# The inner norms of a macaron layer: mean squares by two wide products and an inverse root by exponential and logarithm, in place of narrow sums, a diagonal and a square root

## The chip, the cores and the metric

The kernel runs on one core of one Trainium2 chip. The metric is the device time of one execution in microseconds (us). Engines are named TensorE (PE; its weight loads are PEld), VectorE (DVE), ScalarE (ACT), GpSimd (POOL) and SyncE (SP, which only issues transfers).

## What is computed

One layer over 512 tokens of width 1024, all in float32:

```python
def rmsnorm(x, g):
    y = x * lax.rsqrt(jnp.mean(x * x, axis=-1, keepdims=True) + 1e-6)
    return y * g

x = x + 0.5 * swiglu_ffn(rmsnorm(x, ffn1_norm), ...)      # norm 1, feed-forward width 2816
x = x + hybrid_mixer(rmsnorm(x, mix_norm), ...)           # norm 2, attention and pooling
x = x + 0.5 * swiglu_ffn(rmsnorm(x, ffn2_norm), ...)      # norm 3
x = rmsnorm(x, final_norm)                                # final norm
```

The first three are the inner norms. The final norm is not touched.

## The kernel before

The residual stream is held transposed: eight tiles x[k] of 128 channels by 512 tokens. Products of float32 precision are made of three products in the faster format float32r: each operand is split into a high part (a cast on ScalarE, line 132) and a low part (a subtraction on VectorE, line 133), and mm3 (line 193) adds high x high, high x low and low x high in PSUM. Its lines 198, 199 and 200 are most of TensorE's work.

The work has three stages in a row: the first feed-forward block (about 0 to 325 us), the mix stage (325 to 490) and the second feed-forward block (490 to the end). The feed-forward blocks use a block scheme with seven products instead of eight for most of their work; its sums of weights and of activations run on VectorE, ScalarE and through transfers.

An inner norm never scales x ahead of a product. The products take x times the norm's gain, and what comes out is multiplied per token by the inverse root of the token's mean square. For that the class Norm keeps acc, the sum over k of x[k] squared (128 partitions by 512 tokens: squares on ScalarE, additions on VectorE, lines 308 to 315, for norm 3 the jobs of lines 1695 to 1704). When it is complete:

- per_token (line 317, for norm 2 line 1149): four products of acc with a vector of ones give each token's sum as one column per 128 tokens, tokens on partitions; in float32 each is two instructions, so eight. ScalarE takes the square root (line 326 or 1161), a dummy activation (tables, line 226) loads the table set of the function that comes next, VectorE makes the inverse root r with one Newton step (rsqrt_of, line 285), four columns in all.
- The diagonal (line 332 or 1174): identity times r, 128 by 512.
- spread (line 339 or 1181): ones times the diagonal, two instructions of 512 columns, gives every partition the inverse root of all 512 tokens; ScalarE copies it to rb (line 342 or 1186).

rb is used where channels lie on partitions (gate and up values of the feed-forward blocks, lines 424 and 428; the block scheme's scaled x, line 365; the pooling input, line 1422); r where tokens do (q, k and v, lines 1312 and 1401).

In the feed-forward blocks, ffn_up (line 412) calls norm.finish() with high priority ahead of the last quarter of the products of its first four banks; the compiler's own scheduler orders the engines there. SyncE's transfers, and from line 579 on TensorE, VectorE and ScalarE, follow the written order. The first four banks are evacuated by lines 424 to 428 once rb is there; the blocks of line 397 follow on VectorE.

In the mix stage everything is a job with an engine, a cost, a rank, what it waits for and the banks and buffers that it gets and gives back. plan() (line 1002) replays these costs and writes down the order of every engine. The jobs of norm 2 (lines 1188 to 1193) have rank -1, ahead of nearly all others; line 1491 lets the first of them wait for sixteen products. The Sqrt table for norm 3 is loaded by a job behind the softmax (line 1706).

The dummy activation is what loads a table: an activation whose function isn't in the loaded set gets a load (ACT_TABLE_LOAD) in front.

Of the kernel before, what the change touches and what calls it, by code (L numbers as in the profile page):

```python
# [16 lines left out]
P = 128  # L17
# [14 lines left out]
MAGIC = 1597463007.0  # L32
REL = 257
# [23 lines left out]
def layer(  # L57
# [162 lines left out]
    ones = const.tile([P, P], F32, name="ones")  # L220
    table = const.tile([P, 1], F32, name="table")
    nc.vector.memset(ones, 1.0)
    eps = const.tile([P, 1], F32, name="eps")
    nc.vector.memset(eps, EPS)

    def tables(func, after):

        nc.scalar.activation(table, after, func, scale=0.0)


    tables(AF.Sqrt, ones[:, 0:1])
    idle = abank()
    for _ in range(8):
        nc.tensor.matmul(idle[:, :P], ones, ones, start=True, stop=True)
# [59 lines left out]
    class Norm:  # L294


        def __init__(self, which):
            self.which, self.h, self.acc = which, {}, None
# [9 lines left out]
        def square(self, k):  # L308
            if self.acc is None:
                self.acc = tpool.tile([P, S], F32, tag="acc", name=name("acc"), bufs=1)  # L310
                nc.scalar.activation(self.acc, x[k], AF.Square)
            else:
                sq = temp()
                nc.scalar.activation(sq, x[k], AF.Square)
                nc.vector.tensor_tensor(self.acc, self.acc, sq, op=ALU.add)

        def per_token(self, total, after=None):
            for t in range(NT):
                nc.tensor.matmul(
                    total[:, t : t + 1], self.acc[:, t * P : (t + 1) * P], ones[:, 0:1],  # L320
                    start=True, stop=True,
                )
            v, root, self.r = (
                small.tile([P, NT], F32, tag=what, name=name(what)) for what in ("v", "root", "r")
            )
            nc.scalar.activation(root, total[:, :NT], AF.Sqrt, scale=1.0 / D, bias=eps)
            if after:
                tables(after, root[:, 0:1])
            nc.vector.tensor_scalar(v, total[:, :NT], 1.0 / D, EPS, op0=ALU.mult, op1=ALU.add)
            rsqrt_of(v, root, self.r)  # L330
            self.diag = temp()
            nc.vector.tensor_tensor(
                self.diag.rearrange("p (t c) -> p t c", t=NT),
                ident.unsqueeze(1).to_broadcast([P, NT, P]),
                self.r.unsqueeze(2).to_broadcast([P, NT, P]),
                op=ALU.mult,
            )

        def spread(self, wide):
            nc.tensor.matmul(wide, ones, self.diag, start=True, stop=True)  # L340
            self.rb = small.tile([P, S], F32, tag="rb", name=name("rb"), bufs=1)
            nc.scalar.copy(self.rb, wide)

        def finish(self):
            self.per_token(abank(), AF.Silu)
            self.spread(abank())
# [309 lines left out]
    class Down:  # L656
# [154 lines left out]
        def product(self, acc, g, a, i, further=False, scale=None):  # L811
# [7 lines left out]
            if self.n_products == 12:  # L819
                tables(AF.Sqrt, a[0][:, 0, 0:1].bitcast(F32))  # L820
# [19 lines left out]
    n1, n2, n3 = Norm(0), Norm(1), Norm(2)  # L840
# [100 lines left out]
    with tc.tile_pool(name="mix", bufs=1, reuse_waits="tile") as mpool:  # L941
# [207 lines left out]
        def per_token():  # L1149
            for t in range(NT):  # L1150
                nc.tensor.matmul(
                    buf["total"][:, t : t + 1], n2.acc[:, t * P : (t + 1) * P], ones[:, 0:1],
                    start=True, stop=True,
                )

        n2_small = {}

        def root_of():
            for what in ("v", "root", "r"):
                n2_small[what] = small.tile([P, NT], F32, tag=what, name=name(what))  # L1160
            nc.scalar.activation(
                n2_small["root"], buf["total"][:, :NT], AF.Sqrt, scale=1.0 / D, bias=eps
            )
            tables(AF.Exp, n2_small["root"][:, 0:1])

        def reciprocal_root():
            v, n2.r = n2_small["v"], n2_small["r"]
            nc.vector.tensor_scalar(
                v, buf["total"][:, :NT], 1.0 / D, EPS, op0=ALU.mult, op1=ALU.add
            )  # L1170
            rsqrt_of(v, n2_small["root"], n2.r)

        def diagonal():
            nc.vector.tensor_tensor(
                buf["diag"].rearrange("p (t c) -> p t c", t=NT),
                ident.unsqueeze(1).to_broadcast([P, NT, P]),
                n2.r.unsqueeze(2).to_broadcast([P, NT, P]),
# [3 lines left out]
        def spread():  # L1181
            nc.tensor.matmul(buf["wide"], ones, buf["diag"], start=True, stop=True)

        def spread_copy():
            n2.rb = small.tile([P, S], F32, tag="rb", name=name("rb"), bufs=1)
            nc.scalar.copy(n2.rb, buf["wide"])
# [828 lines left out]
```

## Time and profile before

| what | us |
|---|---|
| median of 3 runs (lowest, highest) | 811.85 (811.62, 812.27) |
| the profiled execution, device time | 811.69 |
| its span, first to last instruction | 809.7 |

The page gives busy time and share of the span for each engine; the chain that ended last is followed back from the last instruction through what released each step. The granted TensorE clock is 0.997 on average, so the clock needs no thought here. Matmuls are pipelined: a row's duration overlaps the next, and the cost of one more is the step from one start to the next. A timeline row has start, duration, engine, line, operation, output <- inputs, shapes, and in brackets the idle time before it with what ended it. A row with "x2" stands for two instructions in a row.

| engine | busy us | share |
|---|---|---|
| TensorE | 797.8 | 99% |
| VectorE | 712.8 | 88% |
| ScalarE | 498.8 | 62% |
| GpSimd | 147.2 | 18% |

### The profile page before, as it was taken

Reading aid. Unit: us, or ns where it says so; the run is one execution under the profiler, and the core shown is the slowest. Engines: PE = TensorE matmul, PEld = TensorE weight load, DVE = VectorE, ACT = ScalarE, POOL = GpSimd, SP = SyncE. Lnnn points to the kernel's source line nnn. Section 1 sums busy time; section 2 is a strip of 40 time slices with the busy share of each in tenths; the row PEclk is TensorE's granted clock in tenths of the full one; section 3 lists DMA queues with packets and bytes.
Section 4 is the critical chain, followed back from the end, with each engine's and each line's share of the span. In section 5 each row is a group of like instructions: output and inputs, shape, how many; then the busy total and the mean of one; then the engine's idle time right before and its main releaser. Section 6 shows DMA issues by size and latency. Waiting matters only on the chain.

```text
span 809.7 us, 14959 instructions
## 1 busy us (share of the span) xinstructions
PE 797.8 (99%) x5730; PEld 749.1 (93%) x5730; DVE 712.8 (88%) x1133; ACT 498.8 (62%) x854; POOL 147.2 (18%) x234
## 2 busy tenths in 40 slices
PE   9999999999999999999999999999999999999995
PEld 8889999999999999888888888899999999988985
DVE  7899999999996997778688788999999999987996
ACT  8446655556666665659659545465666655765683
POOL 0022212223220000100256354111111011100010
PEclk9999999999999999999999999999999999999998
DMA  8276889979999774431599777256666566969642
GB/s 289 76 208 208 237 226 247 216 189 249 248 292 316 220 219 147 142 124 34 156 258 248 196 198 210 80 112 204 172 184 151 163 185 168 272 210 344 211 120 104
DMA packets 73703, 158.56 MB, mean 196 GB/s; under 512 B 6544, under 2 KB 31648, under 8 KB 73248
## 3 DMA queue, kind: packets, MB, share of 16 engines
q1 hardware_dynamic: 49664, 109.09, 40.0%
q0 software_dynamic: 23680, 48.24, 28.3%
q8 instruction: 45, 0.74, 0.4%
q10 hardware_dynamic: 288, 0.27, 0.1%
q14 instruction: 26, 0.21, 0.1%
HBM read 153.38 MB, written 50.34 MB: 252 GB/s over the span
## 4 chain that ended last, share of the span: by engine, by line
PE 91%; DVE 4%; ACT 1%; issue 1%; DVEq 0%; ACTq 0%
PE mm L198 19%; PE mm L200 19%; PE mm L199 19%; PE a L199 10%; PE a L200 9%; PE a L198 9%; PE mm L1605 1%; PE mm L1516 1%; DVE aside L365 1%; PE a L1580 1%; PE mm L1580 1%; DVE aside L371 0%; PE a L1516 0%; DVE parts L133 0%; PE a L1605 0%
## 5 line engine op out<-in xcount | busy, mean ns | idle before, releaser
L571 ACT ACTIVATE t<-mm 128x256 f32<-128x256 f32 x105 | 40.5, 386 | 110.8 <-PE mm L200 108.8
L132 ACT CAST parts<-raw 128x1024 fp32r<-128x1024 f32 (+2 forms) x77 | 74.1, 968 | 54.7 <-PE mm L199 20.5
L133 DVE TENSOR_TENSOR parts<-raw,parts 128x1024 fp32r<-128x1024 f32 (+2 forms) x77 | 85.8, 1121 | 15.1 <-ACT parts L132 14.7
L199 PE MATMUL mm<-ha,parts 128*128 128x256 f32 x280 | 77.0, 275 | 0.0
L200 PE MATMUL mm<-ha,parts 128*128 128x256 f32 x280 | 77.0, 275 | 0.0
L198 PE MATMUL mm<-ha,parts 128*128 128x256 f32 x280 | 77.0, 275 | 0.0
L715 POOL COPY mark<-t 128x1 f32<-128x1 f32 x40 | 15.9, 397 | 330.9 <-DVE t L615 244.8
L717 POOL DMA_DIRECT2D wsum<-in_wB_dram x72 | 71.1, 1123 | 26.1 <-DMA wsum<-wsum 14.1
L482 DVE TENSOR_TENSOR parts<-wsum,parts 128x1024 fp32r<-128x1024 f32 x53 | 64.5, 1217 | 5.1 <-ACT parts L477 5.1
L477 ACT CAST parts<-wsum 128x1024 fp32r<-128x1024 f32 x53 | 53.9, 1047 | 0.6 <-PE mm L200 0.3
L198 PEld LDWEIGHTS mm<-ha,parts 128*128 128x128 f32 x280 | 53.8, 192 | 0.1
L199 PEld LDWEIGHTS mm<-ha,parts 128*128 128x128 f32 x280 | 53.8, 192 | 0.1
L200 PEld LDWEIGHTS mm<-ha,parts 128*128 128x128 f32 x280 | 53.8, 192 | 0.0
L198 PE MATMUL mm<-hhi,parts 128*128 128x512 f32 x128 | 49.6, 391 | 0.2
L200 PE MATMUL mm<-hhi,parts 128*128 128x512 f32 x128 | 48.7, 384 | 0.8 <-DVE parts L133 0.8
L133 DVE TENSOR_TENSOR ah<-acts,ah 128x512 fp32r<-128x512 f32 (+1 forms) x72 | 47.1, 662 | 2.7 <-ACT ah L132 2.4
L199 PE MATMUL mm<-hlo,parts 128*128 128x512 f32 x128 | 48.4, 379 | 0.0
L132 ACT CAST ah<-acts 128x512 fp32r<-128x512 f32 (+1 forms) x72 | 40.9, 580 | 8.8 <-PE mm L199 6.4
L482 DVE TENSOR_TENSOR parts<-raw,parts 128x512 fp32r<-128x512 f32 (+1 forms) x52 | 43.6, 858 | 0.5 <-ACT parts L477 0.5
L500 DVE TENSOR_TENSOR wsum<-raw 128x1024 f32<-128x1024 f32 x35 | 42.6, 1217 | 0.0
L477 ACT CAST parts<-raw 128x512 fp32r<-128x512 f32 (+1 forms) x52 | 39.2, 755 | 4.7 <-DMA raw<-in_wA_dram 3.4
L1122 DVE TENSOR_TENSOR parts<-raw,parts 128x1024 fp32r<-128x1024 f32 x24 | 30.1, 1258 | 11.6 <-ACT parts L1117 11.5
(342 smaller groups left out, 3062.0 us busy)
## 6 DMA issues: line engine op xcount, KB each, us to landing
raw<-in_wA_dram SPq DMA_DIRECT2D x87, 512.0 KB, 4.7
wsum<-in_wB_dram POOLq DMA_DIRECT2D x60, 512.0 KB, 7.5
raw<-wsum SPq DMA_DIRECT2D x36, 512.0 KB, 4.6
raw<-in_wB_dram SPq DMA_DIRECT2D x30, 512.0 KB, 4.9
wsum<-wsum POOLq DMA_DIRECT2D x20, 512.0 KB, 5.0
x<-in_xT_dram SPq DMA_DIRECT2D x16, 256.0 KB, 6.1
raw<-in_wQK_dram SPq DMA_DIRECT2D x8, 512.0 KB, 3.6
wsum<-in_wB_dram POOLq DMA_DIRECT2D x12, 256.0 KB, 5.5
```

The costliest lines, as they stand in the source:

```text
L132: nc.scalar.copy(hi, src)
L133: nc.vector.tensor_tensor(lo, src, hi.bitcast(F32), op=ALU.subtract)
L198: nc.tensor.matmul(acc, a[0], high, start=start, stop=False, **more)
L199: nc.tensor.matmul(acc, a[0], low, start=False, stop=False, **more)
L200: nc.tensor.matmul(acc, a[1], high, start=False, stop=stop, **more)
L477: nc.scalar.copy(hi, src)
L482: nc.vector.tensor_tensor(lo, src, hi.bitcast(F32), op=ALU.subtract)
L500: nc.vector.tensor_tensor(z, raw[:, : 2 * S], raw[:, S : 3 * S], op=ALU.add)
L571: nc.scalar.activation(natural(dst), ordered(src), AF.Copy, scale=scale)
L717: nc.gpsimd.dma_start(self.rows(i, g), self.rows(self.terms[i][at], g), **(dict(accum_op=ALU.add) if at else {}),)
L1122: nc.vector.tensor_tensor(lo, buf["raw", i], hi.bitcast(F32), op=ALU.subtract)
L1580: nc.tensor.transpose(buf["tp", h, group][:, n : n + P], buf["p", h, t][:, j * P : (j + 1) * P], ident,)
```

## The change

Each inner norm gets rb directly. acc is split into a high and a low part, and two products of 512 columns with a constant block of 1/1024 (mean_of) give every partition the mean squares of all tokens. rough() makes y = exp(-0.5 ln(v) - ln 2), half the inverse root, and 4 y y; exact() makes rb = (3 - (v + eps) 4 y y) y, one Newton step. ln and exp are taken from one table set, loaded ahead of time. For norms 1 and 3 a dummy activation that reads y2 then loads the Silu table, between rough() and exact(). For norm 2, r is read back out of rb: identity times rb, reduced along the free dimension. The seven additions of norm 1 go to GpSimd. The diagonal, the spreading product and the copy are gone, and so is the table job behind the softmax. The diff, cut to its core:

```diff
+    mean_of = const.tile([P, P], F32R, name="mean_of")
-    nc.vector.memset(ones, 1.0)
+    nc.vector.memset(mean_of.bitcast(F32), 1.0 / D)
+    less_ln2 = const.tile([P, 1], F32, name="less_ln2")
+    nc.vector.memset(less_ln2, -LN2)
 
     def tables(func, after):
-        nc.scalar.activation(table, after, func, scale=0.0)
-    tables(AF.Sqrt, ones[:, 0:1])
+        if func == AF.Ln:
+            with tc.manual_schedule(engines={mybir.EngineType.Activation}):
+                nc.scalar.copy(table, after)
+                nc.scalar.preload_act_table_set("natural_log_exp_and_others")
+        else:
+            nc.scalar.activation(table, after, func, scale=0.0)
+    tables(AF.Ln, eps)
...
     class Norm:
-        def __init__(self, which):
+        def __init__(self, which, adds):
...
-                nc.vector.tensor_tensor(self.acc, self.acc, sq, op=ALU.add)
+                self.adds.tensor_tensor(self.acc, self.acc, sq, op=ALU.add)
-        def per_token(self, total, after=None):
...
-        def spread(self, wide):
...
+        def mean(self, wide, pair):
+            wide = wide.rearrange("p (i a) -> p i a", a=2)
+            for i in range(2):
+                nc.tensor.matmul(
+                    wide, mean_of, pair[i].rearrange("p (a i) -> p i a", a=2),
+                    start=i == 0, stop=i == 1,
+                )
+        def rough(self, wide, y, y2):
+            nc.scalar.activation(natural(y), ordered(wide), AF.Ln, bias=eps)
+            nc.scalar.activation(y, y, AF.Exp, scale=-0.5, bias=less_ln2)
+            nc.scalar.activation(y2, y, AF.Square, scale=2.0)
+        def exact(self, wide, y, y2):
+            nc.vector.scalar_tensor_tensor(
+                natural(y2), ordered(wide), EPS, natural(y2), op0=ALU.add, op1=ALU.mult
+            )
+            self.rb = small.tile([P, S], F32, tag="rb", name=name("rb"), bufs=1)
+            nc.vector.scalar_tensor_tensor(
+                self.rb, y2, 3.0, y, op0=ALU.subtract, op1=ALU.mult, reverse0=True
+            )
         def finish(self):
-            self.per_token(abank(), AF.Silu)
-            self.spread(abank())
+            wide, y, y2 = abank(), temp(), temp()
+            pair = temp(F32R), temp(F32R)
+            split(self.acc, *pair)
+            self.mean(wide, pair)
+            self.rough(wide, y, y2)
+            tables(AF.Silu, y2[:, 0:1])
+            self.exact(wide, y, y2)
...
-                tables(AF.Sqrt, a[0][:, 0, 0:1].bitcast(F32))
+                tables(AF.Sqrt if self.by_token else AF.Ln, a[0][:, 0, 0:1].bitcast(F32))
...
-    n1, n2, n3 = Norm(0), Norm(1), Norm(2)
+    n1, n2, n3 = Norm(0, nc.gpsimd), Norm(1, nc.vector), Norm(2, nc.vector)
...
+        def mean_high():
+            nc.scalar.copy(buf["sum", 0], n2.acc)
+        def mean_low():
+            nc.vector.tensor_tensor(
+                buf["sum", 1], n2.acc, buf["sum", 0].bitcast(F32), op=ALU.subtract
+            )
...
         def diagonal():
             nc.vector.tensor_tensor(
-                buf["diag"].rearrange("p (t c) -> p t c", t=NT),
-                ident.unsqueeze(1).to_broadcast([P, NT, P]),
-                n2.r.unsqueeze(2).to_broadcast([P, NT, P]),
+                by_token(buf["y"]), by_token(n2.rb), ident.unsqueeze(1).to_broadcast([P, NT, P]),
                 op=ALU.mult,
             )
+        def reduced():
+            n2.r = small.tile([P, NT], F32, name="r")
+            nc.vector.tensor_reduce(n2.r, by_token(buf["y"]), axis=AX.X, op=ALU.add)
...
-        total = z = job("pe", 0.5, -1, per_token, [at_acc], [("bank", "total")])
-        z = job("act", 1.8, -1, root_of, [z])
-        at_r = job("dve", 0.8, -1, reciprocal_root, [z], uses=["total"])
-        z = job("dve", 0.65, -1, diagonal, [at_r], [("t", "diag")])
-        z = job("pe", 0.9, -1, spread, [z], [("bank", "wide")], ["diag"])
-        at_rb = job("act", 0.55, -1, spread_copy, [z], uses=["wide"])
+        pair = [("sum", i) for i in range(2)]
+        z = job("act", 0.6, -1, mean_high, [at_acc], [("m", key) for key in pair])
+        z = job("dve", 0.65, -1, mean_low, [z])
+        total = z = job("pe", 0.45, -1, mean, [z], [("bank", "mean")], pair)
+        z = job("act", 1.8, -1, rough, [z], [("t", "y"), ("t", "y2")])
+        z = at_rb = job("dve", 1.3, -1, exact, [z], uses=["mean", "y2"])
+        z = job("dve", 0.65, -1, diagonal, [z])
+        at_r = job("dve", 0.65, -1, reduced, [z], uses=["y"])
...
-        job("act", 1.5, 6, lambda: tables(AF.Sqrt, ones[:, 0:1]), list(at_prob.values()))
```

More of the change, by code (lines that the diff above doesn't have):

```diff
@@ L32 @@
 MAGIC = 1597463007.0
+LN2 = 0.6931471805599453
 REL = 257
@@ L219, in layer @@
     make_identity(nc, ident)
-    ones = const.tile([P, P], F32, name="ones")
+    mean_of = const.tile([P, P], F32R, name="mean_of")
     table = const.tile([P, 1], F32, name="table")
-    nc.vector.memset(ones, 1.0)
+    nc.vector.memset(mean_of.bitcast(F32), 1.0 / D)
     eps = const.tile([P, 1], F32, name="eps")
     nc.vector.memset(eps, EPS)
+    less_ln2 = const.tile([P, 1], F32, name="less_ln2")
+    nc.vector.memset(less_ln2, -LN2)
     def tables(func, after):
-        nc.scalar.activation(table, after, func, scale=0.0)
-    tables(AF.Sqrt, ones[:, 0:1])
+        if func == AF.Ln:
[5 more added lines that the diff above has]
+    tables(AF.Ln, eps)
     idle = abank()
     for _ in range(8):
-        nc.tensor.matmul(idle[:, :P], ones, ones, start=True, stop=True)
+        nc.tensor.matmul(
+            idle[:, :P], mean_of.bitcast(F32), mean_of.bitcast(F32), start=True, stop=True
+        )
     qk_sb = const.tile([P, 2], F32, name="qk_sb")
@@ L294, in layer @@
     class Norm:
-        def __init__(self, which):
-            self.which, self.h, self.acc = which, {}, None
+        def __init__(self, which, adds):
+            self.which, self.h, self.acc, self.adds = which, {}, None, adds
         def add(self, k, square=True):
@@ L314, in square @@
                 nc.scalar.activation(sq, x[k], AF.Square)
-                nc.vector.tensor_tensor(self.acc, self.acc, sq, op=ALU.add)
-        def per_token(self, total, after=None):
-            for t in range(NT):
+                self.adds.tensor_tensor(self.acc, self.acc, sq, op=ALU.add)
+        def mean(self, wide, pair):
+            wide = wide.rearrange("p (i a) -> p i a", a=2)
+            for i in range(2):
                 nc.tensor.matmul(
-                    total[:, t : t + 1], self.acc[:, t * P : (t + 1) * P], ones[:, 0:1],
-                    start=True, stop=True,
-                )
-            v, root, self.r = (
-                small.tile([P, NT], F32, tag=what, name=name(what)) for what in ("v", "root", "r")
-            )
[L326 to L333, printed above, removed]
-                ident.unsqueeze(1).to_broadcast([P, NT, P]),
-                self.r.unsqueeze(2).to_broadcast([P, NT, P]),
-                op=ALU.mult,
-            )
@@ L1146, in layer @@
             at_acc = job("dve", 0.65, -5, None, [sq, at_acc])
[L1149 to L1162, printed above, removed]
-            )
-            tables(AF.Exp, n2_small["root"][:, 0:1])
@@ L1173, in diagonal, with mean, rough, exact @@
+        def mean():
+            n2.mean(buf["mean"], [buf["sum", i] for i in range(2)])
+        def rough():
+            n2.rough(buf["mean"], buf["y"], buf["y2"])
+        def exact():
+            n2.exact(buf["mean"], buf["y"], buf["y2"])
+        def by_token(z):
+            return z.rearrange("p (t c) -> p t c", t=NT)
         def diagonal():
             nc.vector.tensor_tensor(
-                buf["diag"].rearrange("p (t c) -> p t c", t=NT),
-                ident.unsqueeze(1).to_broadcast([P, NT, P]),
```

14 lines of the change are left out of this document (removed).

## The prediction

> **What bounds the kernel now.** I read the page first, for the busy shares and for the shares of the chain that ended last.
>
> ```profile
> PE 797.8 (99%) x5730; PEld 749.1 (93%) x5730; DVE 712.8 (88%) x1133; ACT 498.8 (62%) x854; POOL 147.2 (18%) x234
> PE 91%; DVE 4%; ACT 1%; issue 1%; DVEq 0%; ACTq 0%
> ```
>
> TensorE is busy for 797.8 us, 99% of the span, and carries 91% of the chain. A microsecond taken from TensorE's stream is therefore a microsecond of time, unless TensorE then stands and waits for another engine. So the second view is what TensorE waited for (engine, tile and line, the releaser, then us in total, times, longest).
>
> ```profile
> PE mm L200 <- DVE parts L133: 0.8, 1, 0.8
> PE mm L198 <- DVE m L1621: 0.6, 1, 0.6
> PE a L319 <- DVE acc L315: 0.4, 1, 0.4
> PE a L1605 <- DVE pTw L1594: 0.3, 1, 0.3
> ```
>
> After the start these are all its waits. Two lie in the first norm's neighbourhood (L319, and L200 behind L133), two in the mix stage (behind L1621 and L1594); nothing is waited for around the third norm. The third view is the chain in order of time (start, us, what), which says which engine carries each norm.
>
> ```profile
> 27.69 0.59 ACT rb L342
> 28.30 0.69 DVE t L424
> ...
> 51.18 1.15 DVE parts L133
> 52.37 0.70 PE mm L200 x2
> ...
> 336.18 0.79 PE a L1151 x8
> ...
> 342.25 0.86 PE a L1182 x2
> ...
> 492.14 0.95 PE a L319 x8
> ...
> 496.22 0.86 PE a L340 x2
> ```
>
> The first norm's row rb starts a run of VectorE work that ends in TensorE's 0.8 us wait at 52.37; the norm's own TensorE work isn't in that stretch. At the second and third norm the chain goes through the norm's TensorE instructions themselves. The busy time by stretches (each engine's busy us and count, then clock, DMA share, GB/s) confirms it.
>
> ```profile
> 28.30:53.00 24.70, 23.93 (x111) 20.61 (x111) 24.65 (x33) 9.77 (x12) 4.49 (x6) 1.00 0.26 86
> 345.00:400.00 55.00, 55.00 (x314) 47.14 (x313) 41.33 (x109) 38.75 (x85) 5.82 (x12) 1.00 0.32 104
> 400.00:450.00 50.00, 48.99 (x284) 41.82 (x283) 43.89 (x116) 38.65 (x86) 26.66 (x37) 1.00 0.84 216
> ```
>
> From 28.30 to 53.00 VectorE (third engine) works 24.65 of 24.70 us. So norm 1 is worth what it shifts the moment at which rb is ready, while norms 2 and 3 are worth what they take from TensorE.
>
> **Norms 2 and 3: TensorE's stream.** Each loses eight narrow products against ones and two passes of a full-precision product against the diagonal, and gains two products with 512 columns in the format of the weight products. What such a product costs is the step between two neighbours in TensorE's timeline.
>
> ```profile
> 495.62 0.38 PE L198 MATMUL mm<-hhi,parts 128*128 128x512 f32 x1
> 495.84 0.38 PE L199 MATMUL mm<-hlo,parts 128*128 128x512 f32 x1
> ```
>
> That step is 0.22 us, so the two new products take 0.44. Norm 2 gives up 0.79 + 0.86 = 1.65 and saves 1.21 us; norm 3 gives up 0.95 + 0.86 = 1.81 and saves 1.37 us. Together 2.58 us, as long as the new chains on ScalarE and VectorE stay hidden. The rows for that cover:
>
> ```profile
> 342.29 0.69 ACT L1312 ACTIVATE t<-mm,r 128x512 f32<-128x512 f32 x1 [0.25 <-PE mm L200]
> 343.01 0.63 ACT L1318 ACTIVATE t<-t 128x512 f32<-128x512 f32 x1
> ...
> 510.15 0.68 DVE L424 TENSOR_TENSOR t<-mm,rb 128x512 f32<-128x512 f32 x1
> ```
>
> At norm 2 the order now is rb first and r after it. The first reader of r (L1312) runs at 342.29. The sums stand at 336.18 as before (the wait behind sixteen products stays); 0.6 for TensorE and the hop, three dependent activations at about 0.7 (342.29 to 343.01 is 0.72 from one to the one that reads it), four VectorE instructions at 0.69 (L424 at 28.30): r at about 336.2 + 0.6 + 2.0 + 2.8 = 341.6, so in time by 0.7 us, or late by half a microsecond if a weight split of 1.2 us stands in between. Late costs nothing either: the evacuated banks are four of eight, and the next four take the value projection meanwhile. At norm 3 the spreading product is over at 497.1, and the first evacuation that reads rb runs at 510.15, when TensorE has finished the first four banks. In between VectorE reads rb only for work that fills its time, so the new chain may lose 1 or 2 us there for nothing. What it can cost is TensorE standing at the new product itself: acc is followed by a copy on ScalarE and a subtraction on VectorE before TensorE may start, some 1.3 us more, while the third norm's place in TensorE's order is fixed when the kernel is built. Bounds 0 to 1 us of standing; I take 0, because before the change the same order left no wait above 0.3 us there. Taking the square-root table load out of the mix stage is worth nothing: it runs on ScalarE, which is busy 38.65 of 50 us there.
>
> **Norm 1: when rb is ready.** ScalarE's and VectorE's timelines (start, us, engine and line, tile, shapes; idle before and releaser in brackets):
>
> ```profile
> 17.88 0.62 ACT L314 ACTIVATE t<-x 128x512 f32<-128x512 f32 x1
> 18.40 1.99 ACT L132 CAST parts<-raw 128x1024 fp32r<-128x1024 f32 x2
> 21.61 1.04 ACT L132 CAST parts<-raw 128x1024 fp32r<-128x1024 f32 x1 [1.21 <-PE mm L199]
> ...
> 23.33 1.28 ACT L228 ACT_TABLE_LOAD   x1
> 24.63 0.20 ACT L228 ACTIVATE table<-root 128x1 f32<-128x1 f32 x1
> ```
>
> ```profile
> 20.09 1.22 DVE L133 TENSOR_TENSOR parts<-raw,parts 128x1024 fp32r<-128x1024 f32 x1
> 21.23 0.68 DVE L315 TENSOR_TENSOR acc<-acc,t 128x512 f32<-128x512 f32 x1
> ```
>
> The last square is done at 18.50, but its addition runs only at 21.23, because VectorE has a weight split of 1.22 us (L133) in front of it. On GpSimd it no longer queues behind that. GpSimd adds of nearly this size exist in the mix stage:
>
> ```profile
> L1430 POOL TENSOR_TENSOR us<-us 128x525 f32<-128x525 f32 x3 | 3.2, 1062 | 0.2
> ```
>
> ```profile
> 418.29 4.42 POOL L1430 TENSOR_TENSOR us<-us 128x525 f32<-128x525 f32 x3
> 419.63 1.93 DVE L1122 TENSOR_TENSOR parts<-raw,parts 128x1024 fp32r<-128x1024 f32 x1
> ```
>
> Alone an add takes 1.06 us; in the run of three beside VectorE's split the worst of them needs 4.42 - 2 x 1.06 = 2.3 us, and the split itself grows from 1.22 to 1.93. So an add costs 1.06 to 2.3; I take 1.6, in the middle, since such a split runs beside a part of the last add. That puts acc at about 18.55 + 1.6 = 20.2 (19.6 to 20.9) in place of 21.91. Nothing else is queued on GpSimd there: its share in the first two slices of the page is nil. The Trainium skill, page "GPSIMD Engine Reference", section "8. Key points", says that GpSimd shares its SBUF interfaces with VectorE and contends with VectorE instructions that have two SBUF inputs, and that elementwise work is structurally about twice as fast on VectorE. The trace agrees on both (1.93 against 1.22; 1.06 against 0.68). By that rule alone the additions would not be moved; what it makes of the time is in the rivals.
>
> From there: ScalarE is free at 20.39, high part 20.4 to 21.0 (0.62, L314). The low part is a VectorE instruction of 0.68; if one more 1.2 us split goes first it ends at 22.3, otherwise at 21.7. TensorE needs 0.6 with the hop: 22.9. Then logarithm, exponential and square, each waiting for the one before: 0.72 + 0.65 + 0.62, so 25.0. (No logarithm or exponential of this shape is in the trace; the activations that are cost 0.62 to 0.69, by L314 and L1312, and I take no other price for the function.) Now the point that the diff hides: the dummy activation that loads the Silu table reads y2, and the first instruction of exact() writes y2. So exact() has to wait until the load (1.28) and the dummy (0.20) are over: 26.5. Two VectorE instructions at 0.69: the first reader of rb starts at about 27.9 instead of 28.30. That is 0.4 us gained. Early (no split ahead of the low part, but ScalarE's cast from 21.61 to 22.65 still ahead of the logarithm) it is 0.7; late (an add of 2.3, the split, and a wider gap at each hop) it is 0.3 lost. I take 0.2 us gained, the middle of the two ends. TensorE's own saving at norm 1 (its 0.4 us wait and, as at norm 3, some 1.4 of work) gives nothing: it only lengthens the wait at 52.37, as VectorE's run of 24.65 us stays the same length. The seven additions taken off VectorE lie before 22 us and give nothing but the earlier acc. The new constants and the first load of the table lie ahead of the first data and cost nothing; at the down-projection's twelfth product one load takes another's place.
>
> The Trainium skill, page "ScalarE: Activation LUTs", section "What ACT_TABLE_LOAD costs", puts a switch of set at 1.28 us plus a drain of about 1.38 us. The rows above show 1.28 and the next activation 0.02 us later, no drain. By the page norm 1 would lose 1.2 us instead of gaining 0.2, and the sum would be 1.4 us.
>
> **Sum.** 0.2 + 1.21 + 1.37 = 2.8 us. The profiled execution took 811.69 us (span 809.7 and 2.0 around it), so it would take 808.9; it lies 0.16 under the median of 811.85. Against the median the forecast is 809.0 us. Its own range, from norm 1's bounds, up to 1 us of standing at norm 3 and 0.3 us of small waits in the mix stage that come or go, is 807.9 to 810.2.
>
> **The rivals.** A measurement of this kernel tells about 0.2% (1.6 us) from no change, so the borders are 810.2 and 813.5.
>
> *exact() isn't held by the table.* If the dummy activation doesn't stand between, rb comes 1.5 us sooner, the 0.8 us wait at 52.37 vanishes with it, and the sum is 2.8 + 1.5 = 4.3: 807.5 us. Against it: the write into y2 must wait for the read in program order.
>
> *Norm 1's chain gets longer than the old one.* Either one more cast (1.04) slips between the three activations, or logarithm and exponential turn out not to share a table and a second load (1.28) stands between them (then the change doesn't do what it says), or the load holds ScalarE longer than in the row when it follows at once on three running activations (the page's drain would be such a case; the row at 24.63 speaks against it), or GpSimd and VectorE slow each other for all seven adds (1.2 us on each of the last ones, 0.7 on a split, by the rows of 418.29 and 419.63). Each moves rb by 1 to 1.3 us: norm 1 costs 1.0, the sum is 1.6, 810.3 us, no change that can be told. For it: the contention is in the rows, and the order of these engines is newly made.
>
> *The mix stage is ordered anew and stands.* The order of all jobs there comes from a planner that replays costs; seven jobs replace six, with other costs, banks and buffers, so every later choice can fall otherwise. Today that stage holds only 0.9 us of listed waits (L1621 and L1605's on L1594, of the 1.0 us that TensorE lacks from 400 to 450), where VectorE has 43.89 of 50 us. A new order that adds 2.8 us of waits eats everything (811.9); from 2.8 + 1.6 = 4.4 us added, five times what is there, the kernel is slower, and with 5 us it takes 814.1. For it: the waits that are left are so small that a changed order has much room to be worse and little to be better. Against it: the new jobs lie in the stage's first fifteen microseconds, and from 345 to 400 TensorE is busy for 55.00 of 55 us with other engines at 41 and 39.
>
> **How the numbers follow.** Forecast 0.52; table doesn't hold 0.10; norm 1 later 0.13; mix reordered 0.25, of which 0.03 still faster, 0.09 within the bound and 0.13 slower. Faster: 0.52 + 0.10 + 0.03 = 0.65. Same: 0.13 + 0.09 = 0.22. Slower: 0.13. The range has to hold the forecast, the second rival and the harmless half of the third: from 807.0, which leaves out a part of the first rival, to 812.4, which leaves out the slower case and a little more.
>
> **What would show it.** Right: two TensorE products instead of ten in each norm, 0.44 us in all; no table load between logarithm and exponential; in norm 1, exact() starting behind the dummy activation, its first reader of rb at 27.6 to 28.6, and TensorE's wait near 52 grown to 2 to 3 us; the step from 340 to 490 shorter by about 1.2 us. Wrong: new TensorE waits in the mix stage of more than 2 us in sum; a TensorE wait on sum's low part at norm 3; rb at 26.5 or at 29.5 in norm 1; GpSimd adds above 2.3 us each.

## The result: slower, and where the time went

The changed kernel takes 817.39 us (median of six, 815.77 to 819.55), the kernel before in the same session 811.94 (six, 811.59 to 812.61). The ratio is 1.0068, with a 95% interval of 1.0051 to 1.0086: slower by 0.7%, or 5.4 us, where 2.8 us of gain were forecast. The profiled execution took 816.09 us (span 814.2), which is 4.4 us above the profiled one of before (811.69).

The page after: busy time of each engine, and the chain's shares by engine.

```profile
PE 797.3 (98%) x5706; PEld 746.7 (92%) x5706; DVE 715.1 (88%) x1120; ACT 501.6 (62%) x857; POOL 157.9 (19%) x241
PE 87%; DVE 6%; ACT 3%; DMA 2%; issue 1%; SPq 0%; POOL 0%; DVEq 0%; ACTq 0%
```

TensorE has the 24 instructions less that were promised (5706 for 5730), yet is busy for only 0.5 us less, and its share of the chain fell from 91% to 87%. VectorE, which has 13 instructions less on balance (seven additions and fifteen small ones are among those gone), is busy for 2.3 us more. What TensorE waits for now (engine, tile and line, releaser, then us in total, times, longest):

```profile
PE a L331 <- ACT t L133: 2.8, 2, 2.1
...
PE mm L199 <- ACT t L584: 0.8, 2, 0.6
PE mm L201 <- DVE parts L495: 0.8, 1, 0.8
```

The new first line is the new product itself: TensorE stands twice, 2.1 us at norm 1 and 0.6 at norm 3, for the high part of the sum (the cast of acc, L133). The 4.4 us can be put in places by comparing times of the same instruction in both traces (the start of the first reader of rb in norm 1, of the first product of the mix stage and of the first product of norm 3's feed-forward block, and the end of the last instruction):

| stretch | before | after | difference |
|---|---|---|---|
| first reader of rb in norm 1 at | 28.30 | 31.79 | +3.49 |
| from there through the first feed-forward block | 296.06 | 297.07 | +1.01 |
| the mix stage, with norm 2 | 163.73 | 163.06 | -0.67 |
| norm 3 to the last instruction of all | 317.80 | 318.39 | +0.59 |

**Norm 1.** GpSimd's timeline, with the additions that were moved to it:

```profile
8.03 1.32 POOL L325 TENSOR_TENSOR acc<-acc,t 128x512 f32<-128x512 f32 x1 [6.23 <-ACT t L324]
...
12.43 9.05 POOL L325 TENSOR_TENSOR acc<-acc,t 128x512 f32<-128x512 f32 x5 [1.41 <-ACT t L324]
```

The last five stand back to back and take 1.81 us each, so acc is complete at 21.48, against 21.91 before. VectorE's timeline over the same time:

```profile
13.47 1.30 DVE L137 SCALAR_TENSOR_TENSOR hlo<-x,gain_sb,hhi 128x512 fp32r<-128x512 f32 x1 [0.40 <-ACT hhi L136]
14.69 2.29 DVE L134 TENSOR_TENSOR parts<-raw,parts 128x1024 fp32r<-128x1024 f32 x1
16.90 3.46 DVE L137 SCALAR_TENSOR_TENSOR hlo<-x,gain_sb,hhi 128x512 fp32r<-128x512 f32 x2
20.29 2.28 DVE L134 TENSOR_TENSOR wlo<-raw,whi 128x1024 fp32r<-128x1024 f32 x1
22.49 0.74 DVE L137 SCALAR_TENSOR_TENSOR hlo<-x,gain_sb,hhi 128x512 fp32r<-128x512 f32 x1
23.15 1.21 DVE L134 TENSOR_TENSOR parts<-raw,parts 128x1024 fp32r<-128x1024 f32 x1
24.28 0.68 DVE L134 TENSOR_TENSOR t<-acc,t 128x512 fp32r<-128x512 f32 x1
...
30.27 0.69 DVE L344 SCALAR_TENSOR_TENSOR t<-a,t 128x512 f32<-128x512 f32 x1 [0.82 <-ACT table L236]
...
31.79 0.69 DVE L437 TENSOR_TENSOR t<-mm,rb 128x512 f32<-128x512 f32 x1
```

While GpSimd adds, a split of 1.22 us takes 2.29 and an hlo of 0.74 takes 1.73. Right after 22.5, with GpSimd idle, the same two forms take 1.21 and 0.74 again. So the low part of the sum (24.28) stands behind a queue that is some 4.7 us longer than it would be (0.56 on the instruction at 13.47, 1.07, twice 0.99 and 1.06 on the next four), while the five additions that it was spared would have cost 5 x 0.6 = 3.0 (a step of 0.6 each, as from 8.35 to 8.96 in the kernel before). ScalarE's timeline shows the rest of the chain:

```profile
21.51 0.62 ACT L133 CAST t<-acc 128x512 fp32r<-128x512 f32 x1 [1.85 <-POOL acc L325]
...
25.82 0.69 ACT L338 ACTIVATE t<-a,eps 128x512 f32<-128x512 f32 x1 [2.73 <-PE a L331]
26.54 0.72 ACT L339 ACTIVATE t<-t,less_ln 128x512 f32<-128x512 f32 x1
27.16 1.03 ACT L133 CAST parts<-raw 128x1024 fp32r<-128x1024 f32 x1
28.10 0.62 ACT L340 ACTIVATE t<-t 128x512 f32<-128x512 f32 x1
28.74 1.28 ACT L236 ACT_TABLE_LOAD   x1
30.04 0.20 ACT L236 ACTIVATE table<-t 128x1 f32<-128x1 f32 x1
```

A weight cast of 1.03 us slipped between exponential and square, and exact() (30.27) starts when the dummy activation has read y2 (30.24). And TensorE, after its 2.1 us of standing, comes back at half speed; its timeline, then the window from 22.20 to 25.50 (busy us and count of each engine, granted clock, DMA share, GB/s):

```profile
22.18 0.79 PE L331 MATMUL a<-t,mean_of 128*128 128x512 f32 x1 [2.12 <-ACT t L133]
22.77 0.63 PE L200 MATMUL mm<-hlo,parts 128*128 128x512 f32 x1
...
25.02 0.76 PE L331 MATMUL a<-t,mean_of 128*128 128x512 f32 x1
```

```profile
22.20:25.50 3.30, 3.30 (x7) 2.31 (x8) 3.30 (x5) 0.88 (x1) 0.00 (x0) 0.50 0.56 164
```

The step between neighbours is 0.43 us in place of 0.22. In the same window of before the clock was 1.00. On rb's own chain this costs little: the second product starts at 25.02, behind a low part that is ready at 24.96, and takes 0.76 where it took 0.39 at the full clock (with the additions on VectorE). From rb on, VectorE's run of 24 us is as long as it was (31.79 to 55.85, before 28.30 to 52.37), so what norm 1 loses goes into the time in full.

**Norm 3.** TensorE's timeline around its two products, and ScalarE's:

```profile
496.67 0.38 PE L200 MATMUL mm<-hlo,parts 128*128 128x512 f32 x1
497.69 0.48 PE L331 MATMUL a<-t,mean_of 128*128 128x512 f32 x1 [0.64 <-ACT t L133]
498.01 0.38 PE L201 MATMUL mm<-hhi,parts 128*128 128x512 f32 x1
...
498.65 0.38 PE L201 MATMUL mm<-hhi,parts 128*128 128x512 f32 x1
499.03 0.48 PE L331 MATMUL a<-t,mean_of 128*128 128x512 f32 x1
499.35 0.38 PE L199 MATMUL mm<-hhi,parts 128*128 128x512 f32 x1
```

```profile
496.07 1.04 ACT L133 CAST parts<-raw 128x1024 fp32r<-128x1024 f32 x1 [1.93 <-DMA raw<-in_wA_dram]
497.02 0.61 ACT L133 CAST t<-acc 128x512 fp32r<-128x512 f32 x1
```

acc was complete at 495.80, but its cast stood behind a weight cast that had waited 1.93 us for a transfer. At a step of 0.22 the first product would have started at 496.89; it starts 0.80 later, takes a step of 0.32, and the second comes 0.16 late and takes 0.32 again: 1.60 us in all, against 1.81 before. The step of 0.32 isn't the price of this product: a weight product that starts behind a wait takes it too (11.20 to 11.52 and 55.85 to 56.17 in the same trace), and the two new products of norm 2, which waited for nothing, took 0.43 together. Of the 1.37 us promised 0.21 are left, and a new wait of 0.28 at 538.55 (for t, L584) takes those.

**Norm 2.** The two products (342.46 to 342.89) cost 0.43 us as forecast. The mix stage as a whole, in windows from its first to its last product, before and after:

```profile
324.36:488.09 163.73, 162.72 (x873) 140.21 (x871) 129.66 (x296) 108.52 (x216) 54.93 (x85) 1.00 0.62 169
```

```profile
328.86:491.92 163.06, 161.99 (x865) 139.35 (x863) 129.88 (x295) 106.76 (x214) 55.44 (x85) 1.00 0.60 169
```

TensorE is idle 1.0 us in both; it works 0.73 us less, not 1.21. In this execution norm 2 thus brings 0.7; in the other traces with the new norm 2 it brings nothing (below).

### The profile page after: what moved, and what is told of

It is laid out like the page before. It is cut to its first block, busy times and chain, and to the rows that moved or that the text cites. A ratio compares the mean times of both kernels' runs of the same rounds, so it can differ in the third digit from the quotient of the medians.

```text
span 814.2 us, 14917 instructions
## 1 busy us (share of the span) xinstructions
PE 797.3 (98%) x5706; PEld 746.7 (92%) x5706; DVE 715.1 (88%) x1120; ACT 501.6 (62%) x857; POOL 157.9 (19%) x241
## 4 chain that ended last, share of the span: by engine, by line
PE 87%; DVE 6%; ACT 3%; DMA 2%; issue 1%; SPq 0%; POOL 0%; DVEq 0%; ACTq 0%
PE mm L201 19%; PE mm L199 19%; PE mm L200 19%; PE a L199 9%; PE a L200 9%; PE a L201 9%; DMA raw<-in_wA_dram 1%; PE a L1612 1%; DMA raw<-in_wO_dram 1%; DVE aside L378 1%; PE a L1587 1%; ACT parts L133 0%; DVE prob L1531 0%; PE mm L1587 0%; DVE aside L384 0%
## 5 line engine op out<-in xcount | busy, mean ns | idle before, releaser
L584 ACT ACTIVATE t<-mm 128x256 f32<-128x256 f32 x105 | 40.4, 385 | 112.8 <-PE mm L201 111.1
L133 ACT CAST parts<-raw 128x1024 fp32r<-128x1024 f32 (+2 forms) x77 | 74.0, 967 | 50.1 <-PE mm L200 16.0
L495 DVE TENSOR_TENSOR parts<-wsum,parts 128x1024 fp32r<-128x1024 f32 x53 | 64.6, 1218 | 4.8 <-ACT parts L490 4.8
L133 ACT CAST ah<-acts 128x512 fp32r<-128x512 f32 (+1 forms) x72 | 40.8, 580 | 8.1 <-PE mm L200 5.7
L495 DVE TENSOR_TENSOR parts<-raw,parts 128x512 fp32r<-128x512 f32 (+1 forms) x52 | 43.4, 859 | 0.0
L1130 ACT CAST parts<-raw 128x1024 fp32r<-128x1024 f32 x24 | 25.2, 1048 | 26.8 <-PE a L200 10.5
```

Of the source, the lines that this page charges most:

```text
L133: nc.scalar.copy(hi, src)
L495: nc.vector.tensor_tensor(lo, src, hi.bitcast(F32), op=ALU.subtract)
L584: nc.scalar.activation(natural(dst), ordered(src), AF.Copy, scale=scale)
L1130: return lambda: nc.scalar.copy(buf["part", i][0], buf["raw", i])
```

## The experiments

The theory after this comparison had three parts. GpSimd and VectorE hold each other up, which costs norm 1 most; the dummy's read of y2 costs about 1.4 us more; and what norms 2 and 3 take from TensorE comes back as standing at the new products and in a newly ordered mix stage. Rivals: the new norm's chain is too long by itself, wherever the additions run; or norms 2 and 3 give their 2.6 us and norm 1 alone eats more. The first four runs take norm 1 apart, the next four put each norm alone into the kernel before, the last three test what was left. The kernel before gave 812.07 (21 runs) beside the first four, 811.99 (33) beside the next four and 811.93 (29) beside the last three.

### Additions back on VectorE

```diff
-    n1, n2, n3 = Norm(0, nc.gpsimd), Norm(1, nc.vector), Norm(2, nc.vector)
+    n1, n2, n3 = Norm(0, nc.vector), Norm(1, nc.vector), Norm(2, nc.vector)
```

> The changed kernel with one edit: the first norm's seven additions stay on VectorE. Theory A (contention: GpSimd's additions beside VectorE's two-input instructions slow both, which makes norm 1's rb late and lets TensorE stand until its clock falls to one half): VectorE's instructions before 22 us go back to 0.75 and 1.22 us, TensorE's steps there stay at 0.22, rb comes 2 us or more earlier than in the changed kernel, and the time falls by 3 to 4.5 us, to 813 to 814.5. Theory B (the longer chain: split, three activations with a cast between them, a table load that holds exact()): whichever engine adds, rb is late; the time stays within 1 us of 817.4.

Measured: 815.55 us (815.22 to 815.86), ratio 1.0040 [1.0028, 1.0053]. That is 1.8 us less than the changed kernel, between the two forecasts. VectorE's splits take 1.22 and its hlo 0.74 again; acc is complete later than with GpSimd (22.2 against 21.5), and the low part still earlier (23.29 against 24.28). The wait at the new product falls to 0.4 us, TensorE keeps its clock, and the first reader of rb runs at 29.73, 2.06 us earlier. 0.80 of these are the weight cast between exponential and square, which no longer comes between them. So the addition is not the long step: what GpSimd's additions do to VectorE's queue is. What is left shows as a wait of TensorE of 1.64 us at 30.47, for the first evacuation that reads rb.

### The dummy activation reads y instead of y2

```diff
-            tables(AF.Silu, y2[:, 0:1])
+            tables(AF.Silu, y[:, 0:1])
```

> The changed kernel with one edit: the dummy activation that loads the Silu table reads y instead of y2, so that exact() need not wait for it (norms 1 and 3). Theory A: norm 1's rb comes about 1.5 us earlier (load and dummy), the rest stays: 815.5 to 816.5. Theory B: the table load is the main part of the lateness: 814 or less. If exact() isn't held by it at all: 817.4.

Measured: 816.9 (814.94 to 817.23), ratio 1.0050 [1.0036, 1.0063]. Alone it is worth little: 0.5 us, within the spread, between theory A's range and no effect. In this trace TensorE stands for 2.1 and then 1.0 us and runs at a clock of 0.50 from 24 to 30 us. The cast between exponential and square (28.12) waits 0.69 us for one of these slow products, and the first reader of rb, ready at 31.75, waits until 32.75 for the product that it reads beside it. While the additions are on GpSimd, something else is late next.

### Both

The two edits above together.

> Both edits together: additions on VectorE and the dummy activation reads y. Theory A: the two gains add, 811 to 813. Theory B: 814 to 816, as the table alone.

Measured: 812.68 (811.79 to 814.64), ratio 1.0012 [1.0003, 1.0021]. Now exact() follows the square and not the dummy. VectorE's timeline with the additions alone moved back, then ScalarE's of the same kernel, then VectorE's with both edits:

```profile
28.20 0.69 DVE L344 SCALAR_TENSOR_TENSOR t<-a,t 128x512 f32<-128x512 f32 x1 [3.10 <-PE mm L201]
...
29.73 0.69 DVE L437 TENSOR_TENSOR t<-mm,rb 128x512 f32<-128x512 f32 x1
```

```profile
26.68 1.28 ACT L236 ACT_TABLE_LOAD   x1
27.97 0.20 ACT L236 ACTIVATE table<-t 128x1 f32<-128x1 f32 x1
```

```profile
26.77 0.69 DVE L344 SCALAR_TENSOR_TENSOR t<-a,t 128x512 f32<-128x512 f32 x1 [1.58 <-ACT t L340]
...
28.29 0.69 DVE L437 TENSOR_TENSOR t<-mm,rb 128x512 f32<-128x512 f32 x1
```

The read of y2 holds rb for 1.44 us. The times lie 2.9 us apart (815.55 and 812.68); in the traces another 1.1 us lie between rb and the end of the first feed-forward block (297.50 and 296.43 in the two traces), and why isn't explained. Norm 1's 3.49 us close with these starts: 31.79 to 29.73 by the additions, 29.73 to 28.29 by the dummy. Together the two edits are worth 4.7 us, one by one 1.8 and 0.5: two causes in a chain, of which the later shows only when the earlier is gone. Even so the first reader runs at 28.29, as before the change (28.30): the new chain without its two faults is exactly as long as the old one.

### The kernel before, with norm 1's additions on GpSimd

```diff
-                nc.vector.tensor_tensor(self.acc, self.acc, sq, op=ALU.add)
+                (nc.vector if self.which else nc.gpsimd).tensor_tensor(
+                    self.acc, self.acc, sq, op=ALU.add
+                )
```

> The kernel before with one edit: the first norm's seven additions go to GpSimd, all else as it was. Theory A: VectorE's instructions beside them double, TensorE waits about 2 us at the sums and runs at half clock after it; rb 2 to 3 us later, 814 to 816. Theory B: no change, 811.5 to 812.5.

Measured: 813.91 (812.89 to 816.13), ratio 1.0023 [1.0014, 1.0032], 1.84 us more than the kernel before, by this edit alone. VectorE's timeline:

```profile
12.32 3.45 DVE L136 SCALAR_TENSOR_TENSOR hlo<-x,gain_sb,hhi 128x512 fp32r<-128x512 f32 x2
15.70 2.30 DVE L133 TENSOR_TENSOR parts<-raw,parts 128x1024 fp32r<-128x1024 f32 x1
...
25.15 0.69 DVE L334 TENSOR_TENSOR t<-ident,r 128x512 f32<-128x512 f32 x1
```

The prices are those of the changed kernel (1.73, 2.30). acc is complete at 20.82, 1.1 us sooner than before, and yet the time is longer. Where it goes is in TensorE's waits:

```profile
PE a L342 <- DVE t L334: 0.8, 1, 0.8
PE mm L200 <- DVE parts L133: 0.8, 1, 0.8
PE a L321 <- POOL acc L315: 0.6, 1, 0.6
```

They lie at 25.90 (for the diagonal), at 18.05 (for a weight split) and at 20.88 (for acc): 2.25 us of standing before 26 us, where the kernel before stood 0.4 for acc; its 0.77 at 52.37 is gone in exchange. So the net is 2.25 - 0.4 - 0.77 = 1.1 us in this trace (its execution, 812.94, is among the fastest of the eleven). The late work is VectorE's, and it reaches TensorE by its own splits. That the two engines hold each other up, and that this costs time, is thus shown without any of the new norm's code. The rest of the theory's forecast did not come: rb is read first at 28.03 (line 367 of this kernel), not 2 to 3 us later, the clock stays at 1.00, and the time stays 0.1 us under the range.

### Each norm alone in the kernel before

Four kernels with `finish()` and the mix stage's jobs in the new form for the norms named and the old form for the others; additions on VectorE, and in norm 1 the dummy reads y. The old form takes its constant from mean_of, with the factor moved to the end.

```diff
         def finish(self):
+            if self.which in (...):      # norms that keep the old form
+                self.per_token(abank(), AF.Silu)
+                self.spread(abank())
+                return
```

> Only norm 1 in the new form, with its additions on VectorE and the dummy activation reading y. Theory A: rb's first reader starts at 28.3 as before (in the kernel with both edits it was 28.29), so nothing is won or lost there: 811.7 to 812.5, and the stretch from 53 to 70 us costs up to 0.5 us through its new order. If norm 1's TensorE saving counted: 810.5.

Norm 1 alone: 811.81 (811.49 to 813.17), ratio 0.9998 [0.9990, 1.0007]; first reader at 28.18.

> Only norm 2 in the new form; the table job behind the softmax stays as it was. Theory A: 1.2 us less work and about 1 us more waits in the mix stage: 811.5 to 812.5. Rival C: 813 to 814, with waits above 2 us in the mix stage.

Norm 2 alone: 812.87 (811.74 to 815.09), ratio 1.0007 [0.9998, 1.0016]. The profiled execution is the slowest of the eleven. TensorE's timeline at its largest wait, then a window of 1 us behind it:

```profile
424.88 2.12 PE L1555 MATMUL a<-m,m 64*128 64x512 f32 x6 [1.76 <-DVE sm L1563]
```

```profile
426.00:427.00 1.00, 1.00 (x8) 0.94 (x6) 1.00 (x9) 1.00 (x5) 1.00 (x3) 0.50 0.95 258
```

The softmax's sum sm is late by 1.76 us, and the clock goes to 0.50 behind it. The kernel before has no wait there. What came late can be followed back: VectorE does the softmax's instructions behind a weight split, which waits for its cast on ScalarE, which waits for the transfer of the weights. The rows of this run, then the same cast in the kernel before:

```profile
421.15 1.05 ACT L1162 CAST parts<-raw 128x1024 fp32r<-128x1024 f32 x1 [3.09 <-DMA raw<-in_wO_dram]
422.24 1.88 DVE L1167 TENSOR_TENSOR parts<-raw,parts 128x1024 fp32r<-128x1024 f32 x1 [3.15 <-ACT parts L1162]
```

```profile
418.54 1.06 ACT L1117 CAST parts<-raw 128x1024 fp32r<-128x1024 f32 x1
```

> Only norm 3 in the new form; the table job behind the softmax stays and loads the set of logarithm and exponential, so the mix stage keeps its plan. Theory A: TensorE does 1.4 us less and stands 0.5 to 0.7 us at the sum's high part: 811.1 to 811.6. If norm 3's later rb or the fuller VectorE costs time: 812 or more.

Norm 3 alone: 811.79 (811.64 to 812.51), ratio 0.9997 [0.9988, 1.0006]. The new product waits 0.4 us, the product behind the first evacuation 0.3, and one of the block scheme's 0.3. Like the run before and the next one, it falls between what the theory and the rival had.

> Norms 2 and 3 in the new form, norm 1 as before (square root, diagonal, additions on VectorE). Theory A (norms 2 and 3 do take TensorE's 1.2 and 1.4 us out, but most of it is eaten on the spot: norm 3 by TensorE standing about 0.6 us for the sum's high part, norm 2 by about 1 us of waits of the newly planned mix stage): 811 to 812, at most 1 us faster than before. Rival C (the newly planned mix stage costs more than norm 2 saves): 812.5 to 814. Had the prediction's sum held: 809.5.

Norms 2 and 3: 812.45 (810.89 to 814.51), ratio 1.0007 [0.9998, 1.0016]; the product of norm 3 waits 0.7.

Against the kernel before, norm 1 alone stands at -0.2 us, norm 3 at -0.2, norm 2 at +0.9 (by the ratio +0.6), each within its interval of no change. Norms 2 and 3 are not worth the 1.21 and 1.37 us forecast for them: both lie outside the intervals. Norm 1's -0.2 is the number forecast, but for another kernel, with its additions on VectorE and a dummy that holds nothing. None of the three makes the changed kernel slow by itself.

### No split at all

Norms 1 and 3 new, norm 2 old, additions on VectorE, the dummy reads y, and one full-precision product instead of copy, subtraction and two fast ones:

```diff
-            pair = temp(F32R), temp(F32R)
-            split(self.acc, *pair)
-            self.mean(wide, pair)
+            nc.tensor.matmul(
+                wide.rearrange("p (i a) -> p i a", a=2), mean_of.bitcast(F32),
+                self.acc.rearrange("p (a i) -> p i a", a=2), start=True, stop=True,
+            )
```

> Norms 1 and 3 in the new form, norm 2 and the mix stage in the old one, norm 1's additions on VectorE, the dummy activation reads y, and the sum of squares is not split: one full-precision product of mean_of with acc (two instructions) in place of copy, subtraction and two fast products. Theory A (the new form loses through the serial copy and subtraction ahead of TensorE's first product, not through TensorE's own work): norm 3 loses its stand at the high part (0.64 us in the changed kernel) and keeps 0.95 us of the old 1.81 - 0.86; norm 1's first reader of rb comes about 1 us sooner than 28.3, at 27.2 to 27.6. Together 810.0 us, ratio 0.9975. Rival B (time at the norms is hidden by what follows, and TensorE's work at norm 3 just turns into another wait): 811.5 to 812, ratio 0.9995 to 1.000, with the first reader early and the wait of TensorE at the end of VectorE's run of 24 us smaller, yet a wait elsewhere.

Measured: 812.01 (810.63 to 812.67), ratio 0.9999 [0.9991, 1.0008]: the rival's time, not the theory's. The stand at norm 3's product is gone, as expected, and a wait of the same size stands behind it; lines of TensorE's waits:

```profile
PE mm L199 <- DVE t L439: 1.3, 1, 1.3
PE mm L201 <- DVE parts L134: 1.3, 2, 0.9
```

The first wait is at 511.31, for the first evacuation that needs rb. It starts at 510.48, 0.33 us later than before, because the new chain (logarithm at 495.21, a weight cast, exponential, square, and the two instructions of exact() apart from each other) has rb ready at 500.5; and TensorE is there 0.87 us sooner. The kernel before had no slack at this place. Its row of the same product:

```profile
510.98 0.45 PE L198 MATMUL mm<-hhi,parts 128*128 128x512 f32 x1
```

The evacuation ahead of it ran from 510.15 to 510.83, so TensorE already came straight behind it, at a step of 0.47 instead of 0.22. What TensorE saves at norm 3 is lost again here, unless the evacuation comes sooner too. At norm 1 the reader comes at 28.03, 0.27 us sooner, not 1, and the wait at the end of VectorE's run (the second row, 0.9) is larger (0.93 against 0.77), not smaller as the rival had it.

### The mix stage ordered anew, with old and with new instructions

In the kernel before, the planner is told another cost for norm 2's inverse root:

```diff
-        at_r = job("dve", 0.8, -1, reciprocal_root, [z], uses=["total"])
+        at_r = job("dve", 2.1, -1, reciprocal_root, [z], uses=["total"])
```

> The kernel before with one number changed: the planner of the mix stage is told that the job making norm 2's inverse root costs 2.1 us on VectorE in place of 0.8. Every instruction is the same, only the order in the mix stage is another. Theory A (a new order of the mix stage by itself moves the time by as much as norm 2's change was to save): a wait of TensorE of 0.5 to 2 us appears somewhere from 415 to 455, time 812.5 to 814. Rival B (the order is worth nothing, and norm 2's new chain itself causes the waits seen with it): within 0.3 us of the kernel before, and the same two small waits in the mix stage.

Measured: 812.39 (811.47 to 813.13), ratio 1.0004 [0.9995, 1.0013]. The time lies between the two forecasts. In the trace the mix stage takes 163.61 us and has the two old waits, so this order is no worse: there the rival holds. The 1.4 us that this execution is longer than the profiled one of before lie in the first feed-forward block (297.47 against 296.06), which the edit doesn't touch.

In the kernel with norm 2 alone, three of the new jobs' costs are changed (products 0.45 to 0.65, rough 1.8 to 2.1, exact 1.3 to 1.4):

> Only norm 2 in the new form, as in the run with norm 2 alone, but the planner is told other costs for three of its seven jobs (products 0.65, the three activations 2.1, the two instructions for rb 1.4, in place of 0.45, 1.8 and 1.3). The same instructions in another order. Theory A (the 1.8 us wait of TensorE on the softmax in the run with norm 2 alone is an accident of that order): the wait at L1555 is gone or another size, time 810.5 to 812. Rival B (norm 2's new chain by itself makes that wait): the wait stays between 1.4 and 2 us, time 812.5 to 813.2.

Measured: 812.75 (812.03 to 814.78), ratio 1.0016 [1.0007, 1.0024]. The 1.76 us wait on sm is gone, and another 1.0 us stands around 379 (0.34 on the softmax's sum and 0.67 on the weights made of it). So the wait isn't part of the new chain as such, but the time did not come down, as the rival had it. Whether the 1.76 us belonged to that order or to that one execution isn't shown: both traces are of the slowest execution of their kernel.

Over all profiled executions the mix stage takes 163.60 to 163.73 us with the old norm 2 (six kernels, one of them newly planned), and 163.06, 163.73, 164.42, 164.61, 165.22, 165.92 and 166.17 with the new one. Four of these seven (164.61 and the three highest) come from executions that were the slowest of their kernels, so their mean overstates it. The other three lie on average at 163.74, where the old form lies: the saving of 1.21 us is missing there too, and one trace shows a part of it. The traces also show what comes late. The weight cast ahead of the softmax waits for the transfer of the output projection's weights (raw<-in_wO_dram) in all seven, from 1.1 us (in the trace with 163.06) to 3.1 (in the one with 166.17), and for no transfer in the six with the old norm 2. Why this transfer is late with the new norm 2 was not isolated.

## Why the prediction was wrong, step by step

- **Norm 1, contention: the step that failed.** The rows of 418.29 and 419.63 held the price (an add up to 2.3, a split 1.93), and the prediction's sum used it for the last add only; the split ahead of the low part stood in it at the undisturbed 1.2. It holds for every pair: an hlo went from 0.74 to 1.73 and a split from 1.22 to 2.29, each about one GpSimd add of 1.06 longer. "The seven additions taken off VectorE ... give nothing" was wrong in sign: five of them took some 4.7 us from VectorE where they gave back 3.0. The rival that named this gave it 1.0 us; the kernel before with this edit alone loses 1.84, the changed kernel 1.8 (against the one with the additions back on VectorE). The prediction's reading that 1.06 against 0.68 agrees with "about twice as fast" was loose: it is a factor of 1.6.
- **Norm 1, acc at 20.2.** It was 21.48, since an add took 1.81 (taken 1.6) and five of them queued. The low part, put at 21.7 to 22.3, ended at 24.96.
- **Norm 1, exact() held by the dummy.** Right as a mechanism, and 1.44 us where isolated; it lay at 30.27 instead of 26.5 because everything ahead of it was late. The cast between two activations, set down as a rival, happened as well (27.16), as long as the additions were on GpSimd.
- **Norm 1, "TensorE's own saving gives nothing".** Right, but not by the wait near 52, which was to grow to 2 to 3 us and was 0.39 (at 55.85). That TensorE would stand 2.1 us and then run at a clock of 0.50 was nowhere in the sum; a mean clock of 0.997 before the change doesn't say what happens behind a new gap.
- **Norm 3, 1.37 us.** The bound of 0 to 1 us of standing was right and the value taken, 0, was not: 0.96 of standing (0.80 and 0.16), and a step of 0.32 for each product instead of 0.22, leave 0.21; the step grew because TensorE started each product behind a wait. The reason given ("the same order left no wait there") was no reason: the old product stood directly behind the sum, the new one behind a cast in ScalarE's queue. That the chain could lose 1 or 2 us for nothing was wrong too: TensorE already came straight behind the first evacuation (510.98), so at that place its saving turns into a wait (511.31 without the split).
- **Norm 2, 1.21 us.** TensorE's two products cost 0.43, as said. r came 19.2 us into the stage (348.1) and not 17.2 (341.6 in the time of before), since the planner put the products about 1.9 us later in it (342.46); nobody on TensorE is seen to wait for it. The gain was lost in the stage behind, where the third rival had put it: +0.9 us with norm 2 alone, where -1.2 was expected, so about 2 us of new waits and slow clock, half of the 4.4 from which that rival decides. The small difference of 0.9 lies within its interval; that the -1.2 is missing doesn't. What every trace with the new norm 2 shows there is ScalarE's wait for the output projection's weights.
- **The first feed-forward block.** 1.0 us was lost between 55 and 70 us (waits of 0.56 and 0.76 on the block scheme's operands, L584 and L495), which no step of the prediction had. From the first reader of rb to the end of that block the traces with the dummy on y took 296.26 to 296.43 (four, before 296.06), the one with the additions alone moved back 297.50; but with norm 1 as before it also varied, from 296.04 to 297.47. Its cause stays open.

By medians, the new form in all three norms costs 0.6 us (both edits), and the two faults 4.7. These two add up to the whole by construction, so they are no second proof.

## What to carry to other kernels

An elementwise operation moved from VectorE to GpSimd beside VectorE work with two operands in SBUF isn't taken off VectorE, as the float32 rows here show: price it as its own duration added to VectorE's queue, for every instruction of the overlap. Before a dummy instruction is given a tile to read, ask who writes that tile next. And a saving in TensorE's instructions counts only after the queues of the casts that feed the new ones have been followed to the instruction ahead of them.

## What the runs showed of the hardware

- The two engines' times add up: 0.74 + 1.06 = 1.80 against 1.73 and 1.81 measured, 1.22 + 1.06 = 2.28 against 2.29. The Trainium skill, page "SBUF — State Buffer", section "Who interferes with whom", calls the shared pair of ports an exclusive lock and says that a VectorE instruction with two inputs in SBUF contends with a GpSimd one that reads SBUF; these rows agree with that.
- TensorE's granted clock fell to 0.50 for 3.4 us behind gaps of 2.12 us (norm 1 in the changed kernel), 1.76 (norm 2 alone) and 0.99 us (both edits; the last two at the softmax, among products of 64 rows, where it fell 0.6 and 2.3 us after the gap). Where the dummy reads y it fell 1.2 us after a gap of 2.13 and stayed for 6.8. It stayed at 1.00 behind a gap of 1.85 us at 12.28 (norm 2 with other costs, among products of 512 columns), one of 1.64 at 30.47 (additions back on VectorE) and one of 1.29 at 511.31 (no split). So the length of the gap alone doesn't decide; what does, no run isolated. The Trainium skill, page "TensorE: Matmul & The Clock Gate", section "What's actually happening", speaks of an activity window of about 3.4 us that runs freely and doesn't start with the work; the 3.4 and 6.8 us at 0.50 fit one such window and two. Its section "HAM oscillation — how this bites in real kernels" gives as the rule no gaps above about 3.4 us; here gaps of 2.12 us and less were enough.
- A product of 512 columns in the fast format took a step of 0.32 instead of 0.22 when it started behind a wait, whichever product it was (497.69 and 55.85 in the changed kernel), and 0.22 when it followed at once, beside products of another operand too (342.46 to 342.89, two products).
